# Softmax row sums of a hybrid attention block: the third pair of each batch is added to the sum tile by an accumulating transfer

## The chip, the cores and the metric

The kernel runs on one core of a Trainium2 chip. The core has a matrix engine (TensorE, "PE" in the profile; its weight loads are listed apart as "PEld"), a vector engine (VectorE, "DVE"), a scalar engine that evaluates activation functions (ScalarE, "ACT"), a general engine (GpSimd, "POOL") and an engine that feeds the DMA queue (SyncE, "SP"). Each engine works through its own instructions in order; between engines, semaphores say what may start. SBUF is the on-chip memory with 128 partitions, PSUM the memory that TensorE writes. The metric is the device time of one execution in microseconds.

## The reference

The reference is one layer of a diffusion backbone on 2048 latent tokens of width 1024 with 256 context tokens. Two head groups share one input projection: grouped-query softmax attention (8 query heads, 2 key heads, head dimension 64) and a bidirectional gated linear recurrence (4 heads of 128). Their outputs are concatenated and projected, and a SwiGLU feed-forward follows. The change is in the softmax attention:

```python
def block(q):
    s = jnp.einsum('bqkgd,bnkd->bkgqn', q, keys).astype(jnp.float32) * scale
    p = jax.nn.softmax(s, axis=-1)
    return jnp.einsum('bkgqn,bnkd->bqkgd', p.astype(vals.dtype), vals)

o = lax.map(block, qb)
```

Every query attends to 256 + 2048 = 2304 keys. The softmax needs, beside the weighted sum of the values, the sum of the exponentials over all 2304 keys, by which the result is divided.

## The kernel before

The kernel runs in stages: modulation vectors, the input projection (until about 730 us), the sweep of softmax attention with the recurrence woven into it (about 730 to 1738 us), the output projection, and the feed-forward in two halves.

The sweep goes through 32 items, one for each of the 16 blocks of 128 queries and each of the two key heads. An item has 4 query heads x 128 queries = 512 columns. For each of the 18 key tiles k of 128 keys, `scores` (lines 1000 and 1001) makes a tile `s` of 128 keys x 512 columns in PSUM with two matmuls, and ScalarE writes its exponentials to SBUF (line 1004, `p<-s`). Two neighbouring key tiles share one buffer `p` of 128 x 1024, a pair; there are six such buffers, and an item makes nine pairs.

Six key tiles, that is three pairs, form a batch (`BATCH = 6`): 32 items x 3 = 96 batches. When the fourth tile of a batch is done, GpSimd adds the first two pairs into the tile `ps` (`add`, line 1011; one buffer). The products of a batch are made at the end of the third step of the next batch (`LAGT = 3`), so two to three steps after the batch's last exponentials: first 12 matmuls with the values (line 1020, `av<-p,VS`), then the row sums (line 1028), in which a block of ones of 32 columns sums over the 128 keys. Line 1028 runs over two tiles: the sum `ps` of the first two pairs, and the third pair `p` as it is. Each is cut into 8 pieces of 128 columns, and four pieces go to four groups of 32 columns of TensorE side by side. All batches of an item add up in the columns 256 to 383 of the PSUM tile `av`, which `drain` empties once per item. In the profile a matmul on fp32 data stands as two records, so 8 products are 16 records.

Between the steps TensorE also makes the row minima for the next item (`mx`, line 969, read by DVE in line 971) and the matmuls of the recurrence (`pa`, line 684, and others). GpSimd works on the recurrence too: elementwise products `Q` (lines 715, 717), `M` (703), `C` (706) and others, on which TensorE and ScalarE wait.

In the sweep the order of TensorE and DVE, and of SyncE at its start, is that of the program text (`manual_schedule`). The order on ScalarE and GpSimd is set by a scheduler that lays the program out ahead of time by its own estimate of durations; waits are inserted where a tile is read or overwritten.

Of the kernel before, what the change touches and what calls it, by code (L numbers as in the profile page):

```python
# [13 lines left out]
ALU = mybir.AluOpType  # L14
AX = mybir.AxisListType

P = 128
# [51 lines left out]
def block_kernel(ctx: ExitStack, tc: tile.TileContext, a: dict, out: bass.AP, dbg=None):  # L69
    nc = tc.nc  # L70
# [78 lines left out]
    with ExitStack() as st:  # L149
# [11 lines left out]
        for j in range(8):  # L161
            wm = wmp.tile([P, KT, 256], F32, tag="wm", name=f"wm{j}")
            nc.sync.dma_start(wm, w_mod_r[:, :, j * 256:(j + 1) * 256])
            if j in DVE_MOD:
                for r in range(2):
# [5 lines left out]
                    for i in range(2):  # L171
                        nc.tensor.matmul(pcol[:, 2 * j + i, r:r + 1], acc[:, i * P:(i + 1) * P], ones,
                                         start=True, stop=True)
                continue
            pm = ps_m.tile([P, 512], F32, tag="mm", name=f"pm{j}", bufs=2)
            for k in range(KT):
                nc.tensor.matmul(pm[:2, :256], sc[:, k, :], wm[:, k, :],
                                 start=(k == 0), stop=(k == KT - 1))
# [33 lines left out]
    with ExitStack() as st:  # L212
# [40 lines left out]
        with ExitStack() as p1:  # L253
            ps_x = pool(p1, "ps_x", 4, PSUM)
            xh = pool(p1, "xh", 2)
            for gr in list(range(1, NTOK // 256)) + [0]:
# [6 lines left out]
                b = (gr + 1) // 2  # L263
                o = (gr - 1) % 2 * 256 if gr else 0
# [18 lines left out]
                for kk in range(KT // 2):  # L283
                    pt = ps_x.tile([P, 512], F32, tag="t", name=f"xT{gr}_{kk}")
                    for i in range(2):
                        for j, xt in enumerate(xs):
                            k = 2 * kk + i
# [3 lines left out]
                    for i in range(2):  # L291
                        k = 2 * kk + i
# [317 lines left out]
    with ExitStack() as st:  # L610
# [327 lines left out]
        NKT = NTOK // P  # L938
        BATCH = 6
        LAGT = 3  # L940

        class Item:
# [65 lines left out]
            def add(self, p):  # L1008

                t = self.sums[p // 3] = op.tile([P, 1024], F32, tag="ps", name=f"ps{self.nm}_{p}")  # L1010
                nc.gpsimd.tensor_tensor(t, self.pairs[p - 1], self.pairs[p], op=ALU.add)  # L1011

            def products(self, k0):

                if k0 == 0:
                    self.av = ps_av.tile([P, 512], F32, tag="av", name=f"av{self.nm}")
                for k in range(k0, k0 + BATCH):
                    for i in range(2):
                        o = k % 2 * 512 + i * 256
                        nc.tensor.matmul(self.av[i * 64:(i + 1) * 64, :256],  # L1020
                                         VS[:, k, self.g * 64:(self.g + 1) * 64],
                                         self.pairs[k // 2][:, o:o + 256],
                                         start=(k == 0), stop=(k == NKT - 1), skip_group_check=True)
                b = k0 // BATCH
                for n, t in enumerate((self.sums.pop(b), self.pairs[3 * b + 2])):
                    for o in range(0, 1024, 512):
                        for i in range(4):
                            nc.tensor.matmul(self.av[i * 32:(i + 1) * 32, 256:384], one32,
                                             t[:, o + i * P:o + (i + 1) * P], start=False,
                                             stop=(b == 2 and n == 1 and o > 0), skip_group_check=True)  # L1030

            def drain(self):
                self.ot = op.tile([P, 256], F32, tag="ot", name=f"ot{self.nm}")
# [18 lines left out]
        one32 = kvp.tile([P, 32], F32, name="one32")  # L1052
# [16 lines left out]
        items = [Item(g * NCH + qt, qt, g) for g in range(2) for qt in range(NCH)]  # L1069
# [28 lines left out]
        for x in range(NKT * NIT + 1):  # L1098
            n, k = divmod(x, NKT)
            item = items[n] if n < NIT else None  # L1100
            if item is None:
                rec.begin(2 * NIT)
                assert not chunks and not rec.lanes and not rec.plan and rec.late is None
                items[-1].products(NKT - BATCH)
                items[-1].drain()
                items[-1].finish(ps_st, "s")
# [59 lines left out]
                items[n - 1].drain()  # L1166
            for m, c in chunks.pop(x, ()):
                items[m].chunk(c)
            if rec.late is not None:
                wait -= 1  # L1170
                if wait <= 0:
                    rec.flush()
# [620 lines left out]
```

## Time and profile before

| what | value |
|---|---|
| median of 3 runs | 3235.79 us (3234.75 to 3237.18) |
| the profiled execution | 3230.49 us, its span 3228.7 us |
| mean granted TensorE clock | 0.993 of full speed |
| PE busy | 3145.3 us, 97% of the span |
| POOL busy | 1575.1 us, 49% |
| DVE busy | 1755.1 us, 54% |
| ACT busy | 1326.6 us, 41% |
| line 1011, POOL, the sums | 96 times, 2395 ns each |
| line 1028, PE, over the sums | 1536 records, 61.9 us |
| line 1028, PE, over the third pairs | 1536 records, 59.5 us |

How to read it: "x" behind an instruction is how often it is there. In the rows of groups, the busy time comes first, then the mean duration of one in ns, then the idle time of the engine just before and what ended it. In rows in order of time, the first number is the start and the second the duration in us; "x24" is a run of 24 merged into one row, and a bracket holds idle time before it and what ended it. Names like `ps<-p,p` give the tile that is written and those that are read, without buffer numbers. The busy time of a group counts overlapping instructions once, but two groups that overlap each other each count the shared time.

### The profile page before, as it was taken

What the parts mean: (1) busy time and instruction counts of PE and PEld (TensorE: products, weight loads), DVE (VectorE), ACT (ScalarE), POOL (GpSimd) and SP (SyncE); (2) the same over time, 40 slices, a digit from 0 to 9 for tenths busy, and PEclk for the clock granted to TensorE, in tenths of its full rate; (3) what the DMA queues carried; (4) which work ended last, traced back from release to release, by engine and by line L of the source; (5) the groups of instructions that cost most, each with busy time, mean ns of one, the idle gap of its engine ahead of it and who ended that gap; (6) DMA issues with size and microseconds to landing.
All of it is one profiled execution on the core that took longest, in us unless ns stands there. A gap on an engine that the chain in (4) does not pass through costs nothing. (4 is left out here: it accounts for less than half of the span.)

```text
span 3228.7 us, 55815 instructions
## 1 busy us (share of the span) xinstructions
PE 3145.3 (97%) x21212; PEld 2559.5 (79%) x21212; DVE 1755.1 (54%) x3070; ACT 1326.6 (41%) x2563; POOL 1575.1 (49%) x1403
## 2 busy tenths in 40 slices
PE   8999999999999999999999999999999999999998
PEld 5998987896777777777777887888877778888886
DVE  6344555416666665665653656445458753333566
ACT  4422222215554555554543225333335443333344
POOL 4322222206767767776634226777600168776222
PEclk9999999999999999999999999999999999999999
DMA  7243544324111211211006435555575533332665
GB/s 246 92 137 125 153 145 146 119 93 121 31 36 46 67 34 49 59 37 48 28 21 201 134 115 183 196 179 189 173 291 195 193 111 115 108 104 98 243 195 185
DMA packets 368999, 406.86 MB, mean 126 GB/s; under 512 B 31285, under 2 KB 260889, under 8 KB 368346
## 3 DMA queue, kind: packets, MB, share of 16 engines
q1 hardware_dynamic: 368730, 403.30, 38.9%
q8 instruction: 166, 2.72, 0.4%
q14 instruction: 103, 0.84, 0.1%
HBM read 273.34 MB, written 129.78 MB: 125 GB/s over the span
## 5 line engine op out<-in xcount | busy, mean ns | idle before, releaser
L971 DVE TENSOR_REDUCE mn<-mx 128x1 f32<-128x512 f32 x496 | 333.9, 685 | 209.7 <-PE mx L969 204.6
L1004 ACT ACTIVATE p<-s 128x512 f32<-128x512 f32 x576 | 338.5, 598 | 167.3 <-PE s L1001 147.5
L1011 POOL TENSOR_TENSOR ps<-p,p 128x1024 f32<-128x1024 f32 x96 | 229.9, 2395 | 162.3 <-ACT p L1004 162.3
L1020 PE MATMUL av<-p,VS 128*64 128x256 f32 x2304 | 268.7, 382 | 0.0
L1000 PE MATMUL s<-qa,K 128*128 128x512 f32 x576 | 253.4, 440 | 10.8 <-ACT p L1004 10.8
L1001 PE MATMUL s<-qb,KB 128*128 128x512 f32 x576 | 227.4, 395 | 0.0
L1020 PEld LDWEIGHTS av<-p,VS 128*64 128x64 f32 x2304 | 158.9, 138 | 82.5 <-issue 13.9
L969 PE MATMUL mx<-K,qa 128*128 128x512 f32 x496 | 200.9, 406 | 2.7 <-DVE mn L971 2.4
L1621 DVE TENSOR_TENSOR dl<-dl,x 128x512 fp32r<-128x512 f32 x154 | 113.7, 761 | 70.8 <-ACT x L1614 69.9
L1000 PEld LDWEIGHTS s<-qa,K 128*128 128x128 f32 x576 | 109.0, 189 | 47.9 <-issue 19.8
L1614 ACT ACTIVATE x<-dl 128x512 fp32r<-128x512 f32 x154 | 96.2, 631 | 106.1 <-DMA dl<-s_hid0A 41.1
L1614 ACT ACTIVATE dh<-dl 128x512 fp32r<-128x512 f32 x154 | 89.0, 623 | 93.7 <-PE pd1A L1682 48.3
L345 PE MATMUL f<-hTh,wh 128*128 128x512 f32 (+1 forms) x320 | 120.8, 377 | 6.9 <-ACT ft L374 6.9
L969 PEld LDWEIGHTS mx<-K,qa 128*128 128x128 f32 x496 | 93.4, 188 | 41.4 <-DVE mn L971 17.8
L1621 DVE TENSOR_TENSOR dl<-dl,dh 128x512 fp32r<-128x512 f32 x154 | 102.0, 688 | 43.1 <-ACT dh L1614 42.0
L122 POOL TENSOR_TENSOR rs_xf<-ms_xf,mhalf 128x1 f32<-128x1 f32 x16 | 12.7, 803 | 227.6 <-DVE ms_xf L120 227.6
L345 PE MATMUL f<-hTh,wl 128*128 128x512 f32 (+1 forms) x320 | 118.5, 370 | 0.0
L345 PE MATMUL f<-hTl,wh 128*128 128x512 f32 (+1 forms) x320 | 118.4, 370 | 0.0
L1001 PEld LDWEIGHTS s<-qb,KB 128*128 128x128 f32 x576 | 109.6, 190 | 10.9
L1445 PE MATMUL pA<-x,A22h 128*128 128x512 f32 x352 | 108.9, 391 | 4.5 <-DVE r L1518 4.5
L1445 PE MATMUL pA<-x,A11h 128*128 128x512 f32 x352 | 110.7, 395 | 2.4 <-ACT A11h L1414 2.4
L1445 PE MATMUL pC<-x,A12h 128*128 128x512 f32 x352 | 112.0, 391 | 0.0
(373 smaller groups left out, 9337.0 us busy)
## 6 DMA issues: line engine op xcount, KB each, us to landing
w<-in_w_gu_dram SPq DMA_DIRECT2D x88, 512.0 KB
wm<-in_w_mod_dram SPq DMA_DIRECT2D x24, 1024.0 KB
dl<-s_wT SPq DMA_DIRECT2D x88, 256.0 KB
dl<-s_wB SPq DMA_DIRECT2D x66, 256.0 KB
wq<-in_w_down_dram SPq DMA_DIRECT2D x44, 256.0 KB
s_wT<-wq SPq DMA_DIRECT2D x44, 256.0 KB
dl<-s_hid1S SPq DMA_DIRECT2D x44, 256.0 KB
dl<-s_hid0S SPq DMA_DIRECT2D x44, 256.0 KB
```

Source lines behind the costliest of these rows:

```text
L122: nc.gpsimd.tensor_tensor(rs, ms, mhalf[:, :width], op=ALU.pow)
L345: nc.tensor.matmul(pm[:, :n], w[wi][:, k, c0:c0 + P], hT[b][hi][:, k, :], start=(k == 0 and i == 0), stop=(k == KT - 1 and i == 2))
L969: nc.tensor.matmul(s, self.qa[:, h * P:(h + 1) * P], K[:, k * 512:(k + 1) * 512], start=True, stop=True)
L971: nc.vector.tensor_reduce(self.mn[:, h, k:k + 1], s, axis=AX.X, op=ALU.min)
L1000: nc.tensor.matmul(s, KS[self.g][:, ks], self.qa, start=True, stop=False)
L1001: nc.tensor.matmul(s, KB[k // BATCH][:, k % BATCH * P:(k % BATCH + 1) * P], self.qb, start=False, stop=True)
L1004: nc.scalar.activation(self.pairs[p][:, o:o + 512], s, AF.Exp, scale=-1.0)
L1011: nc.gpsimd.tensor_tensor(t, self.pairs[p - 1], self.pairs[p], op=ALU.add)
L1020: nc.tensor.matmul(self.av[i * 64:(i + 1) * 64, :256], VS[:, k, self.g * 64:(self.g + 1) * 64], self.pairs[k // 2][:, o:o + 256], start=(k ...
L1445: nc.tensor.matmul(acc, w[wi][:, k, :], x[xi][k], start=(start and k == 0 and i == 0), stop=(stop and k == KH - 1 and i == 2), skip_group_ ...
L1614: nc.scalar.activation(hi, f32v(lo), AF.Copy)
L1621: nc.vector.tensor_tensor(lo, f32v(lo), f32v(hi), op=ALU.subtract)
```

## The change

The third pair of each batch is no longer multiplied with ones by itself. Instead an accumulating transfer, issued from GpSimd's queue, adds it to the sum tile `ps` in SBUF: `ps += p`, 128 partitions x 1024 fp32 values, 512 KB. The products with ones then run over the one tile `ps`. The transfer is issued in the program text at the end of the first step of the next batch (`k % BATCH == 0`), and for the last batch of all just ahead of its products.

```diff
+            def add_last(self, p):
+
+                t = self.sums[p // 3]
+                nc.gpsimd.dma_start(t, self.pairs[p], accum_op=ALU.add)
+
             def products(self, k0):
...
                 b = k0 // BATCH
-                for n, t in enumerate((self.sums.pop(b), self.pairs[3 * b + 2])):
-                    for o in range(0, 1024, 512):
-                        for i in range(4):
-                            nc.tensor.matmul(self.av[i * 32:(i + 1) * 32, 256:384], one32,
-                                             t[:, o + i * P:o + (i + 1) * P], start=False,
-                                             stop=(b == 2 and n == 1 and o > 0), skip_group_check=True)
+                t = self.sums.pop(b)
+                for o in range(0, 1024, 512):
+                    for i in range(4):
+                        nc.tensor.matmul(self.av[i * 32:(i + 1) * 32, 256:384], one32,
+                                         t[:, o + i * P:o + (i + 1) * P], start=False,
+                                         stop=(b == 2 and o > 0), skip_group_check=True)
...
+                items[-1].add_last(NKT // 2 - 1)
                 items[-1].products(NKT - BATCH)
...
             for m, c in chunks.pop(x, ()):
                 items[m].chunk(c)
+            if k % BATCH == 0 and x:
+                items[(x - 1) // NKT].add_last((x - 1) % NKT // 2)
```

The places that count are the products with ones on TensorE and the sums on GpSimd. First TensorE, at the second batch of the 16th item (in the profile of before the one whose products with the values start at 1206.06 us). The rows give line, operation, tile written, tiles read and shape; the last number in a name is a running number, "x8" stands for eight instructions in a row. Before:

```order
L684 MATMUL pa_13692<-Q_12532,M_6_13577 64x64 x8
L1020 MATMUL av_0_13536<-p_0_3_13483,VS 64x256 x4
L1020 MATMUL av_0_13536<-p_0_4_13511,VS 64x256 x4
L1020 MATMUL av_0_13536<-p_0_5_13608,VS 64x256 x4
L1028 MATMUL av_0_13536<-ps_0_4_13591,one_7838 32x128 x8
L1028 MATMUL av_0_13536<-p_0_5_13608,one_7838 32x128 x8
L1000 MATMUL s_0_15_13759<-qa_0_12771,K_7830 128x512
```

And TensorE with the change at the same place (its lines are five further down in the file):

```order
L684 MATMUL pa_13371<-Q_12273,M_6_13255 64x64 x8
L1025 MATMUL av_0_13222<-p_0_3_13168,VS 64x256 x4
L1025 MATMUL av_0_13222<-p_0_4_13197,VS 64x256 x4
L1025 MATMUL av_0_13222<-p_0_5_13286,VS 64x256 x4
L1033 MATMUL av_0_13222<-ps_0_4_13269,one_7838 32x128 x8
L1000 MATMUL s_0_15_13430<-qa_0_12498,K_7830 128x512
```

Eight matmuls are gone; the others stand as before, and the products over `ps` directly behind those with the values, ahead of the next scores. Now GpSimd at the same batch, whose sum tile is `ps_0_4`, before:

```order
L665 TENSOR_TENSOR Q_13826<-q_13598,F_13596 128x512 x2
L1011 TENSOR_TENSOR ps_0_4_13591<-p_0_3_13483,p_0_4_13511 128x1024
L703 TENSOR_TENSOR M_3_13617<-M_2_13600,T_1_13606 128x16x2x4
L706 TENSOR_TENSOR C_3_13618<-M_2_13600,T_1_13606 128x16x8
L706 TENSOR_TENSOR C_4_13636<-M_3_13617,T_2_13623 128x8x16
L703 TENSOR_TENSOR M_4_13635<-M_3_13617,T_2_13623 128x8x2x8
```

And GpSimd with the change:

```order
L665 TENSOR_TENSOR Q_13498<-q_13276,F_13274 128x512 x2
L1011 TENSOR_TENSOR ps_0_4_13269<-p_0_3_13168,p_0_4_13197 128x1024
L703 TENSOR_TENSOR M_3_13295<-M_2_13278,T_1_13284 128x16x2x4
L706 TENSOR_TENSOR C_3_13296<-M_2_13278,T_1_13284 128x16x8
L1016 DMA ps_0_4_13269<-p_0_5_13286 128x1024
L706 TENSOR_TENSOR C_4_13314<-M_3_13295,T_2_13301 128x8x16
L703 TENSOR_TENSOR M_4_13313<-M_3_13295,T_2_13301 128x8x2x8
```

The transfer (line 1016) is a new row; here it stands two rows behind its sum, in 55 of the 96 batches directly behind it, and at most three rows of other work lie between. The recurrence's rows around it have moved by a few places at most.

## The prediction

> **What bounds the kernel now.** I read the page first (busy shares, slices, queues), then the stretch of the softmax sweep alone, then the groups of the two lines that the change touches, and last four neighbouring batches in order of time. The page:
>
> ```profile
> span 3228.7 us, 55815 instructions
> PE 3145.3 (97%) x21212; PEld 2559.5 (79%) x21212; DVE 1755.1 (54%) x3070; ACT 1326.6 (41%) x2563; POOL 1575.1 (49%) x1403
> PE   8999999999999999999999999999999999999998
> POOL 4322222206767767776634226777600168776222
> q1 hardware_dynamic: 368730, 403.30, 38.9%
> ```
>
> TensorE is busy in nine tenths of nearly every slice, GpSimd in six or seven tenths of the slices of the sweep (10th to 22nd). The only queue with data on it is the one that SyncE feeds: no transfer in this profile was issued by GpSimd, so the new instruction has no row of its own. The sweep, and in it the products with ones:
>
> ```profile
> 730.00:1738.00 1008.00, 981.89 (x10077) 732.57 (x10078) 600.90 (x1073) 519.81 (x1048) 683.62 (x718) 0.99 0.19 54
> 730.00:1738.00 1008.00, 103.77 (x3072) 77.99 (x3072) 0.99 0.19 54
> L1028 PE MATMUL av<-ps,one 128*32 128x128 f32 x1536 | 61.9, 279 | 0.0
> L1028 PE MATMUL av<-p,one 128*32 128x128 f32 x1536 | 59.5, 273 | 0.0
> L1011 POOL TENSOR_TENSOR ps<-p,p 128x1024 f32<-128x1024 f32 x96 | 229.9, 2395 | 162.3 <-ACT p L1004 162.3
>   POOL ps L1011: 0.4, 1
> ```
>
> The first row counts every engine (PE, PEld, DVE, ACT, POOL), the second only line 1028. The sweep has 96 batches in 1008 us, 10.5 us each, and TensorE works in 981.89 us of it: it sets the pace, and what is taken from it is gained. The last row is from the list of what line 1028 waited for: the products with ones waited for the sum in one batch of 96, for 0.4 us. The sum is on time, then, but a busy bar does not say by how much; that is the question here.
>
> **The change, part by part.**
>
> Removed: per batch one group of 16 recorded matmuls with ones, over the third pair. Its row says 59.5 us, but it overlaps the group over the sum: both together cover 103.77 us, the sum's group alone 61.9, so 103.77 - 61.9 = 41.9 us go. The time order gives the same from another side (rows below): in the batch at 1199 us the second group begins 0.46 us after the first (1199.25, 1199.71), as in the three others, and the next scores follow both at the same pitch; 96 x 0.46 = 44 us. I take 44, all of it on TensorE, which nothing hides. The dropped weight loads run beside the matmuls and count in it.
>
> Added: 96 transfers of 512 KB (128 partitions x 1024 fp32), which add the third pair onto the sum in SBUF. Each waits for two things, the end of the sum of the first two pairs (POOL, line 1011) and the exponentials of the batch's sixth tile (ACT, line 1004); and the products with ones, which now follow the transfer, stand on TensorE in the old place. So what counts is the room between the later of these two and the first product with ones. Four batches, with the rows that end each:
>
> ```profile
> 1191.00 2.40 POOL L1011 TENSOR_TENSOR ps<-p,p 128x1024 f32<-128x1024 f32 x1 [3.40 <-ACT p L1004]
> 1191.84 1.29 ACT L1004 ACTIVATE p<-s 128x512 f32<-128x512 f32 x2 [0.99 <-PE s L1001]
> ...
> 1199.25 0.64 PE L1028 MATMUL av<-ps,one 128*32 128x128 f32 x16
> 1199.71 0.62 PE L1028 MATMUL av<-p,one 128*32 128x128 f32 x16
> ...
> 1203.23 2.38 POOL L1011 TENSOR_TENSOR ps<-p,p 128x1024 f32<-128x1024 f32 x1
> ...
> 1206.06 2.76 PE L1020 MATMUL av<-p,VS 128*64 128x256 f32 x24
> ...
> 1208.75 0.65 PE L1028 MATMUL av<-ps,one 128*32 128x128 f32 x16
> ...
> 1214.19 2.42 POOL L1011 TENSOR_TENSOR ps<-p,p 128x1024 f32<-128x1024 f32 x1
> ...
> 1219.62 0.65 PE L1028 MATMUL av<-ps,one 128*32 128x128 f32 x16
> ...
> 1222.07 2.37 POOL L1011 TENSOR_TENSOR ps<-p,p 128x1024 f32<-128x1024 f32 x1 [1.32 <-ACT p L1004]
> ...
> 1224.59 0.59 ACT L1004 ACTIVATE p<-s 128x512 f32<-128x512 f32 x1
> ...
> 1231.54 0.65 PE L1028 MATMUL av<-ps,one 128*32 128x128 f32 x16
> ```
>
> First batch: sum done at 1191.00 + 2.40 = 1193.40, exponentials at 1193.13, products at 1199.25: room 5.85 us. Second: sum done 1205.61, products 1208.75: 3.14. Third: 1216.61 to 1219.62: 3.01. Fourth: here the exponentials are last, 1225.18, products 1231.54: 6.36. The mean is 4.6 us. The 24 matmuls of line 1020 (2.76 us) lie inside the room already. A transfer that takes L from the moment it may go to the moment the products may start costs, in each batch, L minus the room, if that is positive; TensorE's queue is in order, so all scores behind it slip by as much. I take the four for the 96 (times 24).
>
> What is L? The nearest rows are a load of the same 512 KB by SyncE into SBUF, at a quiet moment, its issue in order of time and then the windows (DMA share and GB/s are the last two columns):
>
> ```profile
> 768.01 0.33 SPq L643 DMA_DIRECT2D F<-s_f  x1
> 768.00:768.90 0.90, 0.52 (x6) 0.44 (x8) 1.00 0.00 0
> 768.90:770.50 1.60, 1.60 (x18) 1.06 (x16) 1.00 0.87 210
> 770.50:771.50 1.00, 0.64 (x6) 0.14 (x2) 1.00 0.49 197
> 771.50:772.00 0.50, 0.00 (x0) 0.00 (x0) 1.00 0.00 0
> ```
>
> The load is issued at 768.01 us; nothing moves until 768.90, and all has moved by 771.50: 0.9 us to the first byte and 2.6 us of movement, 3.5 in all. That is the lower end, a transfer that only copies. An accumulating one has two operands to fetch per element, its source and the sum; twice the movement is 5.2 us. The issue is bounded below by the same 0.9 us, above by the longest thing that GpSimd does with a tile of this size here, 2.4 us (line 1011). So L lies between 0.9 + 2.6 = 3.5 and 2.4 + 5.2 = 7.6, and more if the adding itself is slow. [...]
>
> [...]
>
> Lateness at L = 6.6: 0.75 + 3.46 + 3.59 + 0.24 = 8.04 us in four batches, 193 us in 96. At the ends: L = 3.5 gives 0.36 + 0.49 = 0.85, 20 us; L = 7.6 gives 12.04, 289 us.
>
> GpSimd's queue: 96 issues of 1.4 us are 134 us, 683.62 + 134 = 818 us of a sweep that gets 149 us longer (1157): 71%, still not the bound. In the order the transfer stands right behind its sum in 55 of the 96 batches, and the recurrence's work (Q, M, C) behind it, which waits through the issue and, as in the fourth batch, for 0.74 us of exponentials. TensorE's and ScalarE's recurrence steps wait for that work. The waiting of TensorE at the sums, some 2 us a batch, lets GpSimd catch up by about what the issues cost it, so I cost both at nothing together; if it caught up fully, the room would be that to the exponentials alone in the second and third batch too. The other way, an uncovered 1.4 us in every batch, is 134 us more at most.
>
> Single edits with one answer: the third pair's buffer is held until the transfer has read it, but TensorE read it last before, in the same place, and the products still follow; the sum's one buffer is free earlier or later only with the products; the stop flag moves to the last product and costs nothing. [...] SyncE's order is the same there but for a few rows at the sweep's end, and behind the sweep the order of work stays as it was.
>
> Sum: -44 + 193 = +149 us. The profiled execution took 3230.5 us, so 3379 for it; the median of the runs before is 5.3 us above it, 3235.8, and the forecast for the median is 3385.
>
> **The rivals.**
>
> *The transfer is hidden and the gain stays.* It needs L below 3.9 us: there the lateness, (3.9 - 3.14) + (3.9 - 3.01) = 1.65 times 24, is 40 us and nearly eats the 44. For it speaks the room of 5.85 and 6.36 in half the batches and the 3.5 us of the load; against it the second operand. At L = 3.5 the time is 3236 - 44 + 20 = 3212; where the second and third batch find a quicker GpSimd too, 3192.
>
> [...]
>
> *The adding is slow.* If the engines need longer than for two reads, say L = 9, the lateness is 3.15 + 5.86 + 5.99 + 2.64 = 17.6 a group of four, 423 us, and the time 3236 - 44 + 423 = 3615. No row speaks for or against it; only the other 512 KB transfers, all plain, lie at 2.6 us of movement.
>
> *GpSimd becomes the bound.* Per batch it works 683.62 / 96 = 7.1 us, and TensorE, relieved, (1008 - 44) / 96 = 10.0. An issue above 2.9 us on GpSimd would make its queue the pace. At 4 us, L is 9.2, the lateness 442 us and the time about 3634. The longest pass over such a tile (2.4 us) speaks against it.
>
> **How the numbers follow.** The forecast (L from 4.1 to 8): 0.61, own range 3242 to 3519. Hidden (faster): 0.13. Between them, L from 3.8 to 4.1, within 0.2%, which is about what a measurement of this kernel can tell from no change: 0.04. Slow adding: 0.18. GpSimd the bound: 0.04. Faster 0.13, same 0.04, slower 0.61 + 0.18 + 0.04 = 0.83. The range leaves out the hidden case and the far end of the slow ones: 3230 to 3630.
>
> **What would show it.** Right: the group av<-p,one is gone from TensorE, line 1028's cover falls by some 42 us, and the products with ones wait for a DMA into ps in most batches, some 2 us each, near 190 us together; scores and exponentials keep their durations; the sweep lasts some 1150 us and all other stages stay. Wrong: if these waits are a few us in total (hidden), if they average 4 us and more (slow adding), or if TensorE waits for Q or M of the recurrence instead and GpSimd's bar stands near ten tenths (its queue). What would make it wrong is above all the one number without a row, the time of an accumulating transfer.

## The result and the profile after

The changed kernel takes 3360.08 us (median of 4 runs, 3355.32 to 3366.92) against 3235.27 us before, measured beside it: a ratio of 1.0387, 95% interval 1.0372 to 1.0402, or 125 us more. The prediction was 3385 us. The profiled execution has a span of 3353.5 us at a granted clock of 0.980 (0.993 before). The page of the kernel after:

```profile
span 3353.5 us, 53042 instructions
PE 3144.7 (94%) x19676; PEld 2546.1 (76%) x19676; DVE 1761.7 (53%) x3070; ACT 1328.3 (40%) x2563; POOL 1655.0 (49%) x1499
PE   8999999988988889889888999999999999999998
q0 software_dynamic: 13824, 50.34, 8.0%
```

TensorE has 1536 records less and is yet busy as long as before (3144.7 us against 3145.3), so what is left became slower. The loss lies in the 9th to 22nd slices, the sweep, where eights stand among the nines. A new queue carries 50 MB, GpSimd's. The sweep alone, all engines and then line 1033 (the products with ones, line 1028 before):

```profile
730.00:1866.00 1136.00, 983.17 (x8563) 721.35 (x8563) 608.67 (x1074) 521.87 (x1049) 762.97 (x814) 0.96 0.41 93
730.00:1866.00 1136.00, 65.58 (x1536) 37.75 (x1536) 0.96 0.41 93
```

The sweep is 128 us longer (1136 against 1008), the whole of the loss. TensorE's idle time in it rose from 26.1 us (1008 - 981.89) to 152.8 (1136 - 983.17). What it waited for, from the list of waits of TensorE in the sweep (total us, times, longest), and the sources of those waits, from the groups by line and the transfers' own row:

```profile
PE av L1033 <- DMA ps<-p: 123.0, 63, 5.0
...
PE s L1000 <- ACT p L1004: 3.1, 3, 2.5
...
PE pk L732 <- POOL M L703: 2.0, 3, 1.0
```

```profile
L1016 POOL DMA_DIRECT2D ps<-p x96: 730/876/1065, 739.5 to 1851.6; - x96
DMA to landing us min/median/max: 4.4/4.8/8.6
```

The products with ones wait for the transfer in 63 of 96 batches, 2.0 us each; nothing else on TensorE's list is near. The issue holds GpSimd 0.88 us (the middle of the three durations, in ns), and the data has landed 4.8 us after it began. One batch in order of time, the same as the second of the prediction's four (there the sum began at 1203.23 and the products at 1208.75):

```profile
1272.88 2.37 POOL L1011 TENSOR_TENSOR ps<-p,p 128x1024 f32<-128x1024 f32 x1
1273.82 0.60 ACT L1004 ACTIVATE p<-s 128x512 f32<-128x512 f32 x1 [0.17 <-PE s L1001]
1275.04 2.76 PE L1025 MATMUL av<-p,VS 128*64 128x256 f32 x24
...
1275.62 0.46 POOL L706 TENSOR_TENSOR C<-M,T 128x128 f32<-128x128 f32 x1
1276.02 0.86 POOL L1016 DMA_DIRECT2D ps<-p  x1
1280.62 0.66 PE L1033 MATMUL av<-ps,one 128*32 128x128 f32 x16 [2.82 <-DMA ps<-p]
1281.21 0.80 PE L1000 MATMUL s<-qa,K 128*128 128x512 f32 x1
1281.80 0.63 PE L1001 MATMUL s<-qb,KB 128*128 128x512 f32 x1
```

The sum is done at 1275.25, the exponentials before that; the transfer is issued at 1276.02, behind work of the recurrence, and the products follow 4.60 us later, after 2.82 us in which TensorE had nothing to do. And the scores behind them, here 0.80 and 0.63 us, took about 0.4 us each at this place before. The windows around the batch, engine PE alone (busy, clock, DMA share, GB/s), tell why:

```profile
1277.60:1281.10 3.50, 0.68 (x18) 1.00 0.70 131
1281.10:1284.50 3.40, 3.40 (x16) 0.50 0.01 2
1284.50:1288.00 3.50, 2.53 (x14) 1.00 0.48 135
```

In the 3.4 us behind the wait TensorE is granted half its clock (the figure 0.50 in the second row). In the trace's clock record of the whole sweep there are 25 such stretches after, 99.0 us together, and 4 before (13.7 us). Each lasts 3.41 us or twice that. So the transfer costs twice: the wait, and then a stretch at half speed.

TensorE wasn't idle all through the time ahead of this stretch: in the first of these windows it worked for 0.68 of 3.50 us.

### The profile page after: what moved, and what is told of

Its sections match the earlier page's. It is cut to its first block, busy times and chain, and to the rows that moved or that the text cites. A ratio compares the mean times of both kernels' runs of the same rounds, so it can differ in the third digit from the quotient of the medians.

```text
span 3353.5 us, 53042 instructions
## 1 busy us (share of the span) xinstructions
PE 3144.7 (94%) x19676; PEld 2546.1 (76%) x19676; DVE 1761.7 (53%) x3070; ACT 1328.3 (40%) x2563; POOL 1655.0 (49%) x1499
## 5 line engine op out<-in xcount | busy, mean ns | idle before, releaser
L1000 PE MATMUL s<-qa,K 128*128 128x512 f32 x576 | 264.1, 459 | 3.1 <-ACT p L1004 3.1
L1001 PE MATMUL s<-qb,KB 128*128 128x512 f32 x576 | 236.5, 411 | 0.8 <-DMA qb<-mr 0.8
L969 PE MATMUL mx<-K,qa 128*128 128x512 f32 x496 | 207.9, 420 | 2.7 <-DVE mn L971 2.4
L1033 PE MATMUL av<-ps,one 128*32 128x128 f32 x1536 | 65.6, 291 | 123.1 <-DMA ps<-p 123.0
L1033 PEld LDWEIGHTS av<-ps,one 128*32 128x32 f32 x1536 | 37.7, 112 | 164.6 <-DMA ps<-p 157.3
L1453 PE MATMUL pB<-x,S1h 128*128 128x512 f32 x352 | 110.9, 396 | 2.3 <-ACT S1h L1422 2.3
```

The costliest lines, as they stand in the source:

```text
L969: nc.tensor.matmul(s, self.qa[:, h * P:(h + 1) * P], K[:, k * 512:(k + 1) * 512], start=True, stop=True)
L1000: nc.tensor.matmul(s, KS[self.g][:, ks], self.qa, start=True, stop=False)
L1001: nc.tensor.matmul(s, KB[k // BATCH][:, k % BATCH * P:(k % BATCH + 1) * P], self.qb, start=False, stop=True)
L1453: nc.tensor.matmul(acc, w[wi][:, k, :], x[xi][k], start=(start and k == 0 and i == 0), stop=(stop and k == KH - 1 and i == 2), skip_group_ ...
```

## Experiments

Four causes were open: the wait for the landing, the clock behind it, the work of GpSimd and its queue, and a gain smaller than the 44 us expected. In the tables below "half clock" is the sum of the half-clock stretches of the sweep in the profiled execution. Where a kernel leaves out or changes part of the sum, its exponentials have another scale (line 1004, `scale=-0.01` for `-1.0`), which changes no shape and no order. Differences in time are taken from the run of the kernel before that was measured beside each kernel (medians of 3232.67 to 3235.27 us). Where a kernel needs a tile more, the result `oo` is written over `ot` to make space; those lines aren't shown.

### The gain alone

```diff
-                items[-1].add_last(NKT // 2 - 1)
...
-            if k % BATCH == 0 and x:
-                items[(x - 1) // NKT].add_last((x - 1) % NKT // 2)
```

> The changed kernel without the transfer: the third pair of each batch is left out of the row sums, and the exponentials are taken with a hundredth of the scale (so that no sum is zero); all other work is as in the changed kernel. Theory A (the loss is the wait for the transfer's landing, and the slower clock behind long waits): the 42 us of the dropped products show in full, about 3193 us (3185 to 3202), no waits at the products with ones, and no more half-clock stretches in the sweep than the 4 of before. Rival B (the dropped products never were worth their time, because TensorE then waits for the recurrence on GpSimd): 3215 us or more, with waits for Q, M or C.

Measured: 3210.15 us, ratio 0.9928 (0.9913 to 0.9942), between the times of the two expectations. The dropped products are worth 24 us, not 44. The sweep, and new waits in it, of TensorE's weight loads and then of its matmuls:

```profile
730.00:1718.00 988.00, 951.56 (x8563) 696.65 (x8561) 605.21 (x1077) 517.54 (x1049) 681.79 (x718) 0.99 0.19 55
```

```profile
PEld pk L732 <- POOL M L703: 10.1, 3, 3.4
...
PE pk L732 <- POOL M L703: 8.8, 3, 2.9
```

The sweep is 20 us shorter. TensorE's busy time fell by 30.3 us (981.89 to 951.56), and its idle time rose by 10.3 (26.1 to 36.4), 8.8 of them in three waits for the tiles `M` of the recurrence: work that is off TensorE brings it sooner to these tiles, which GpSimd makes at its old pace (646 ns each on the mean, 649 before). Of the missing busy time (the group covered 41.9 us) some 5 us are the clock, an estimate: half of the 10.2 us by which the half-clock stretches rose (13.7 to 23.9). The rest isn't settled.

This run is also the base for the others: between it and the changed kernel, with the same 8563 records on TensorE, the sweep is 148 us longer, 116 us idle and 32 us of the same work done slower.

### The landing, by size

`half`, and `quarter` with 256 for 512:

```diff
-                nc.gpsimd.dma_start(t, self.pairs[p], accum_op=ALU.add)
+                nc.gpsimd.dma_start(t[:, :512], self.pairs[p][:, :512], accum_op=ALU.add)
```

> The accumulating transfer moves 256 KB instead of 512 KB: only the first half of the third pair is added, the second half is left out of the sums, and the exponentials are taken with a hundredth of the scale. Theory A1 (most of the 4.8 us to landing is movement of two operands): the landing falls to about 3.3 us, the waits at the products from 157 us to some 50, the time to about 3245 us (3220 to 3270). Theory A2 (most of it is a fixed cost of issue and completion): landing about 4.3 us, waits above 110 us, 3310 us or more. Rival B (GpSimd's queue, which the issue holds up): no change against the changed kernel if the issue stays at 0.88 us, 3350 to 3360.

> As the accumulating transfer of 256 KB, but 128 KB: a quarter of the third pair is added (the rest left out, a hundredth of the scale). 512 KB landed after 4.8 us, 256 KB after 3.4 us. If landing is a fixed part plus movement in proportion (2.0 + 1.4 per 256 KB): 2.7 us, and the time falls by half of the last step or a little less, to 3275 to 3295 us; what is then left above 3210 us is not movement but issue, completion and GpSimd's queue. If there is a floor under 256 KB: landing 3.2 us or more and 3295 to 3310 us.

| bytes | issue, us | landing (median), us | time, us | ratio (95%) | wait at the products, us | half clock, us |
|---|---|---|---|---|---|---|
| 512 KB (the changed kernel) | 0.88 | 4.8 | 3360.08 | 1.0387 (1.0372 to 1.0402) | 123.0 in 63 batches | 99.0 |
| 256 KB (`half`) | 0.88 | 3.4 | 3306.43 | 1.0222 (1.0207 to 1.0237) | 54.9 in 31 | 78.5 |
| 128 KB (`quarter`) | 0.88 | 2.7 | 3280.89 | 1.0141 (1.0121 to 1.0162) | 42.9 in 22 | 71.7 |

The issue costs GpSimd the same at every size; the landing is 2.0 us and 1.4 us more per 256 KB. The landing came out as the first theory of `half` had it, but the time lies outside its range, 3220 to 3270 us; `quarter` fell into its range. The time follows the landing: 124.8, 71.9 and 47.5 us above the kernel before. The first of these steps holds something else too: the smaller transfers read only the fifth tile of the batch, not the sixth, so they wait for less and are issued sooner (0.79 us behind the end of the sum on the mean, against 1.08). The second step has the size alone, and it is 35 us for each us of landing ((71.9 - 47.5) / 0.7). Carried on to 2.0 us, a transfer without data, that would be 23 us above the kernel before still, where the kernel without transfers lies 24 below: an estimate, but it says that some 45 us hang on something other than the size.

### A copy in place of the adding, from two queues

The sum goes to a tile of its own, and the transfer copies it to the tile that the products read: the same bytes and place in the program, but nothing is added. The copy waits for the sum only, not for the exponentials of the sixth tile. `plain_sp` issues it from SyncE (`nc.sync`).

```diff
-                t = self.sums[p // 3] = op.tile([P, 1024], F32, tag="ps", name=f"ps{self.nm}_{p}")
+                t = self.sums[p // 3] = op.tile([P, 1024], F32, tag="pu", name=f"pu{self.nm}_{p}")
...
-                t = self.sums[p // 3]
-                nc.gpsimd.dma_start(t, self.pairs[p], accum_op=ALU.add)
+                u = self.sums[p // 3]
+                t = self.sums[p // 3] = op.tile([P, 1024], F32, tag="ps", name=f"ps{self.nm}_{p}")
+                nc.gpsimd.dma_start(t, u)
```

> The transfer copies instead of adding: from GpSimd's queue, 512 KB from the sum of the first two pairs into a second tile, over which the products with ones run; the third pair is left out of the sums, and the exponentials are taken with a hundredth of the scale. The product of item output is written over its own input tile to make room for the second tile. It waits for the sum only, not for the sixth exponentials. Theory A1 (reading a second operand and adding costs most): landing near the 3.5 us of the SyncE load, waits some 50 us, time about 3240 us (3215 to 3265). Theory A2 (issue and completion from this queue cost most): landing 4.3 us or more, time above 3310 us.

> As the copying transfer of 512 KB from GpSimd's queue (third pair left out of the sums, a hundredth of the scale), but issued by SyncE. Theory A (landing against room): SyncE's transfer lands in about 3.0 us too, so the waits stay near those of the copy from GpSimd, 3265 to 3295 us. Rival B (the instruction on GpSimd's queue, 0.6 us, and what it holds up): without it the time falls below 3250 us.

Measured: 3285.36 us from GpSimd's queue, ratio 1.0154 (1.0137 to 1.0171), and 3239.50 us from SyncE's, 1.0020 (1.0009 to 1.0030). The transfer's row and the products' wait, from GpSimd:

```profile
L1017 POOL DMA_DIRECT2D ps<-pu x96: 567/593/767, 739.9 to 1784.8; - x96
...
DMA to landing us min/median/max: 2.9/3.0/8.6
```

```profile
PE av L1034 <- DMA ps<-pu: 57.1, 35, 3.9
```

And from SyncE:

```profile
PE av L1034 <- DMA ps<-pu: 27.7, 26, 2.4
```

Both times lie outside what the first theory of each gave; the second of `plain_sp` held. Without the adding the same 512 KB land in 3.0 us, not 4.8, and 74 of the 125 us are gone. Not all 74 are the landing's: the copy is also issued sooner, 0.68 us behind the end of the sum on the mean where the adding transfer takes 1.08, which at 35 us for each us is an estimate of 14 us, and its issue is shorter (0.59 us for 0.88). The packets show the difference in landing: in the trace's records one of 4 KB takes 0.340 us when it is added and 0.162 us when it is copied (medians).

Issued by SyncE the copy costs 44 us less (50.8 - 6.8). Some 29 of them are shorter waits at the products (57.1 to 27.7). Where the products waited, they came 3.0 us behind the issue in both runs (medians 3.03 and 3.05), so the landing is no quicker; but from GpSimd the issue came 0.68 us behind the end of the sum on the mean, from SyncE 0.09. On GpSimd it stands in one order with the sums and the recurrence's work. The other 15 can't be put to one wait. No accumulating transfer was issued from SyncE, so whether the change itself could go that way wasn't tried.

### The transfers without the wait

The kernel of the first experiment, and 96 accumulating transfers of the same size and place into a tile of zeros that nobody reads:

```diff
-                t = self.sums[p // 3]
-                nc.gpsimd.dma_start(t, self.pairs[p], accum_op=ALU.add)
+                nc.gpsimd.dma_start(spare_sum, self.pairs[p], accum_op=ALU.add)
```

> The kernel without the transfer (third pair left out of the sums, a hundredth of the scale), and beside it the 96 accumulating transfers of 512 KB from GpSimd's queue, now into a tile that nobody reads, so that no engine but GpSimd's own next transfer waits for a landing (an item's output is written over its input tile to make room). The run without the transfer took 3210 us. Theory A (the loss is the wait for the landing and the clock that it slows): 3210 to 3222 us. Rival B (the issue on GpSimd's queue and the recurrence's work held up behind it are a good part of the loss): 3235 us or more, with waits of TensorE for Q, M or C. The copy of 512 KB took 46 us more from GpSimd's queue than from SyncE's, which speaks for a part of B.

Measured: 3250.11 us, ratio 1.0046 (1.0034 to 1.0058), so 41 us more than without the transfers (16.7 above the kernel before, not 24.4 below), though no product waits for a landing. The sweep, two of TensorE's waits in it, and a group of GpSimd, in that order:

```profile
730.00:1749.00 1019.00, 959.65 (x8549) 701.43 (x8548) 605.57 (x1073) 516.04 (x1047) 757.75 (x814) 0.97 0.45 102
```

```profile
PEld s L1000 <- ACT p L1004: 27.5, 25, 4.3
...
PE s L1000 <- ACT p L1004: 19.2, 12, 3.9
```

```profile
L703 POOL TENSOR_TENSOR M<-M,T 128x256 f32<-128x256 f32 (+1 forms) x120 | 84.0, 700 | 0.8 <-DVE T L721 0.7
```

The same group without transfers (`no_transfer`):

```profile
L703 POOL TENSOR_TENSOR M<-M,T 128x256 f32<-128x256 f32 (+1 forms) x120 | 77.5, 646 | 1.5 <-DVE T L721 1.4
```

GpSimd is busy 76 us longer than without the transfers (757.75 to 681.79). That is the issues, 0.87 us each at the middle, and slower rows, such as the products `M`, which take 700 ns instead of 646; the two overlap in part. TensorE meets it later and at other places, above all as scores that wait for ScalarE (19.2 us where the run without transfers has 11.5). Of the 41 us, 31 lie in the sweep: 23 idle and 8 of slower work (59.4 - 36.4, 959.65 - 951.56). Which of the two, the issues or the slower rows, weighs more stays open. A third is in this run too, the traffic: the DMA engines are busy for 0.45 of the sweep instead of 0.19, and ScalarE and GpSimd wait 12 us more for the loads of `F` (17.4 and 7.7 us, 10.6 and 2.1 without transfers). No run parts it from the others, so the 41 us are those of the transfers apart from the wait, not shown to be GpSimd's alone. They are close to the 45 us that the sizes left over.

### More room for the transfer

The products with ones are made three steps later, with two sum tiles; `drain` and `finish` move by as much. `before_room3` is the same move in the kernel before, without the transfer.

```diff
-                t = self.sums[p // 3] = op.tile([P, 1024], F32, tag="ps", name=f"ps{self.nm}_{p}")
+                t = self.sums[p // 3] = op.tile([P, 1024], F32, tag="ps", name=f"ps{self.nm}_{p}", bufs=2)
...
+            def row_sums(self, k0):
...
-            if k == 3 and n:
+            if k == 6 and n:
                 items[n - 1].drain()
...
-            if k == 5 and n:
+            if k == 8 and n:
                 items[n - 1].finish(ps_h, "h")
...
+            y = x - 5 - BATCH
+            if k % BATCH == 5 and y >= 0:
+                items[y // NKT].row_sums(y % NKT)
```

> The changed kernel's whole computation, with its products with ones three steps later (at the end of the sixth step of the next batch instead of the third, two sum tiles instead of one, the emptying of the item three steps later as well; the item's output is written over its input tile to make room). Theory A (landing against room): three steps are some 3 us more room, so nearly all waits at the products go, with them the long gaps and the half-clock stretches; time 3190 to 3215 us, below the kernel before. Rival B (the issue on GpSimd's queue and what it holds up behind it): the queue is as it was, so the loss stays, above 3300 us.

> The kernel before, whole, with its products with ones three steps later, as in the run that moves them in the changed kernel (two sum tiles, the emptying of an item three steps later, the output written over its input tile). If moving the products is itself free: 3230 to 3240 us, and the 3255 us of the moved changed kernel are the transfer's own cost. If the later products or the later emptying cost by themselves: 3250 us or more, and the remaining loss there is not the transfer's.

Measured: 3255.55 us with the transfer, ratio 1.0072 (1.0054 to 1.0091); 3241.38 us for the kernel before with the same move, 1.0026 (1.0015 to 1.0037). Waits of TensorE with the transfer:

```profile
PE av L1035 <- DMA ps<-p: 18.2, 20, 2.5
...
PE pk L732 <- POOL M L703: 15.9, 3, 5.3
```

None of the expected times was met. The same transfer, landing as late (4.7 us), loses 104 of its 125 us when the products come three steps later. So the wait, with the half clock behind it (41.0 us of it left for 99.0), was the cause of most of it. But the kernel doesn't become faster than before: of the 21 us left the move itself costs 9 (by the second run), and the transfer 12 beyond that, though the dropped products bring 24. If these parts simply add, that is a cost of some 36 us with most of the waits gone, the third figure beside the 45 and the 41; 18.2 us of waits are still in it.

### The clock

If the half clock comes from TensorE's idle time, work that nobody needs, put into that time, should bring the clock back. `filler` puts 32 unread matmuls (some 1.8 us) ahead of the products with ones in the 19 batches with the longest gaps, `filler2` 56 of them (`range(14)`) in 42 batches.

```diff
+                if 3 * self.n + b in FILL:
+                    for j in range(8):
+                        for i in range(4):
+                            nc.tensor.matmul(self.av[i * 32:(i + 1) * 32, 384:512], one32, VS[:, 0, :],
+                                             start=False, stop=False, skip_group_check=True)
```

> The changed kernel, whole, with 32 further matmuls of 128 columns (some 1.8 us), whose results nobody reads, ahead of the products with ones in the 19 batches whose gap on TensorE was 2.4 us or more. If the half-clock stretches come from the length of those gaps: the gaps fall below 2.8 us, the half-clock stretches of the sweep from 25 to 8 or fewer, and the time falls by 20 to 40 us although work was added, 3320 to 3340 us. If the clock has nothing to do with the gaps: as many stretches as before and 3360 us or more.

> The changed kernel, whole, with 56 further matmuls of 128 columns (some 3.2 us), whose results nobody reads, ahead of the products with ones in the 42 batches whose gap on TensorE was 1.2 us or more. The first such run cut the gaps by 1.8 us and left the half-clock stretches; in the traces each stretch follows a fixed window of 3.41 us in which TensorE was busy for less than about half. If the clock goes by that busy share: nearly no window falls below it, and the half-clock stretches of the sweep go from 25 to 6 or fewer; the added work costs about 40 us where the gap was shorter than it, the clock gives back about 30: 3350 to 3380 us. If the stretches stay at 20 or more, the share is not what sets them.

Measured: 3371.33 us, ratio 1.0420 (1.0399 to 1.0442), and 3397.04 us, 1.0501 (1.0469 to 1.0532). With the first, 24 stretches were left of 25: the length of the gap, on which it was built, was a poor reading. In the traces of before and after, the clock record changes only on a fixed grid of 3.41 us. Laid against it, the stretches of the kernel before followed windows in which TensorE was busy for 0.32 to 0.34 of the time, and the lowest window that led to none had 0.57. In the changed kernel the two overlap: of the windows at full clock, those that led to one had up to 0.52, and the lowest that led to none had 0.41. In the sweeps of all runs every window at full clock below 0.40 led to a stretch and none above 0.55 did; between them it went either way. A window that itself ran at half clock could lead to another at more, up to 0.84 (in `half`). So the busy share of the window is what the stretches go by as far as the traces show, but it alone doesn't fix a boundary. By that reading a gap of 2.8 us that is split evenly between two windows may do nothing (it leaves 0.59 of each, an estimate from 1.4 of 3.41 us), and a filling of 1.8 us, 0.53 of a window, may not lift one that holds little else far enough. The second run, with more, left 13 stretches (47.8 us for 99.0), more than expected, in a time above the expected range; but for one that went on from a half-clock window, they followed windows of 0.53 and less. That agrees with the reading but doesn't prove it. Neither kernel gained: in the second TensorE is busy 117.5 us longer in the sweep and idle only 78.5 us less, so the unread work is longer than the idle time that it fills and the clock that it gives back.

### The adding on another engine

```diff
-                nc.gpsimd.dma_start(t, self.pairs[p], accum_op=ALU.add)
+                nc.vector.tensor_tensor(t, t, self.pairs[p], op=ALU.add)
```

The call stands just ahead of the products. `dve_late` does this in the last 5 of the 32 items only (15 batches, with 32 of the recurrence's `Q`, `M` and `C` products left on GpSimd) and leaves the others as in the kernel before.

> The third pair is added onto the sum tile by VectorE (one elementwise addition of 128x1024 per batch, standing just ahead of the batch's products) instead of by the transfer; the products are those of the changed kernel and the whole result is computed. Theory A (what lost the time is the landing, not the dependence on a second addition): an addition on VectorE takes some 1.2 us by the two of that shape in the next stage (1.23 us), less than the 2.8 us of products that cover it, so the time comes near that of the kernel without the transfer, 3205 to 3230 us, below the kernel before. Rival (a later sum is bad in itself, because VectorE waits for GpSimd's sum and the minima behind it are held up): 3240 us or more.

> The kernel before, whole, but in the last 5 of the 32 items (15 batches), where little of the recurrence is left on GpSimd, the third pair is added to the sum tile by VectorE ahead of the products, and those run over one tile; the other 27 items are as before. If the dropped products pay wherever the addition is off the engines that are needed: 15 x (24 / 96 to 42 / 96 us) = 4 to 7 us less, 3226 to 3230 us against 3233. If the addition on VectorE costs there too: 3233 us or more.

Measured: 3249.25 us, ratio 1.0048 (1.0030 to 1.0067), which is the time that the rival gave, and 3231.92 us, 0.9998 (0.9986 to 1.0009), no difference that shows (the interval leaves room for a gain of 4 us, not of 7). In the first:

```profile
730.00:1752.00 1022.00, 961.72 (x8557) 701.27 (x8557) 728.69 (x1171) 512.03 (x1048) 749.45 (x718) 0.98 0.19 53
```

```profile
L715 POOL TENSOR_TENSOR Q<-Q,T 128x256 f32<-128x256 f32 x96 | 101.0, 1052 | 75.9 <-PE pa L684 75.8
```

And the same group without the adding (`no_transfer`):

```profile
L715 POOL TENSOR_TENSOR Q<-Q,T 128x256 f32<-128x256 f32 x96 | 66.7, 694 | 80.9 <-PE pa L684 80.9
```

VectorE has the time for it (busy 728.69 of 1022 us). But GpSimd, with the same 718 instructions as without the adding, is busy 749.45 us instead of 681.79; its products `Q` take 1052 ns instead of 694. The trace tells where: the 43 of them that overlap an addition on VectorE in time took 1481 ns, the other 53 705. Why they took longer, the trace doesn't show. TensorE is idle 24 us longer than in `no_transfer`; 15.5 of them are scores that wait for ScalarE (27.0 us, 11.5 there), and 7.3 are products that wait for the addition itself, in 9 batches. So this way too is paid for, for the most part away from the products; that it goes through the recurrence's path is argued from GpSimd's longer rows. No version tried that makes the whole sum beats the kernel before by more than the noise.

## Why the prediction was right, and where not

The sign, the mechanism (products that wait for a DMA into `ps`) and the time within 25 us held. The terms did so less well, and the nearness is in part luck: the waits were taken 70 us too long, and a gain taken 20 us too large and two terms that were missing made up for most of it.

| term | predicted, us | shown, us | by |
|---|---|---|---|
| products gone | -44 | -24 | `no_transfer` |
| waits for the landing | +193 | 123 | the list of waits after |
| GpSimd's issues and its queue | 0 | about +40, traffic included | `side_transfer`, also `room3`, the sizes |
| clock behind the waits | not in the sum | at most 32 of slower work, some 8 of it in the line above | windows of the sweep |
| sum | +149 | +125 | the runs |

The terms shown are measured in different runs and overlap, so they don't add up to the last line. From `no_transfer` on, the loss is 124.8 + 24.4 = 149 us, of which 41 come with transfers that nobody waits for; if the rest is the wait, 108 belong to the waiting and the clock behind it.

**The room.** The step that took four batches for 96, with the room between the later of sum and exponentials and the first product, was sound. With the L that the trace shows, about 0.5 us from ready to issue (the median) and 4.8 to the landing, 5.3 us together, the prediction's own formula gives (5.3 - 3.14 + 5.3 - 3.01) x 24 = 107 us; the rooms of all batches in the trace of before give 111 us, in 57 batches, so the four were a fair sample. 123 were measured, in 63 batches rather than 48.

**L.** The term that was mis-sized is L, 6.6 us taken: 1.4 us until the first byte and 5.2 of movement, twice the load's 2.6. These were estimates; no run of before shows a transfer from GpSimd's queue or one that adds. The first part measured 1.45 us from the issue; but the issue came 0.5 us behind the moment at which it could go, and the landing is told 0.34 us behind the end of the last packet, two parts that the estimate had no term for. The second had about the right factor (0.340 us for a packet that is added against 0.162 for one that is copied; what in the adding takes the time, no run shows) but the wrong base: the 2.6 us were those of a load from HBM, and the copy inside SBUF from this queue moved in 1.5 us (from its first byte, 1.17 us after the issue, to the end of its last packet). The movement took 3.0 us where 5.2 were taken:

```profile
1276.00:1276.90 0.90, 0.90 (x3) 1.00 0.02 1
1276.90:1277.60 0.70, 0.70 (x3) 1.00 0.50 94
1277.60:1280.40 2.80, 2.80 (x7) 1.00 0.88 164
1280.40:1281.00 0.60, 0.60 (x3) 1.00 0.00 0
```

These are windows of the kernel after, engine POOL, with DMA share and GB/s last, for the transfer issued at 1276.02.

**The gain.** "All of it on TensorE, which nothing hides" failed: 24 us came of 44. Of the 20 that are missing, the trace of `no_transfer` gives 8.8 to TensorE's waits for GpSimd's `M` and some 5 to the half clock; the rest stays open. That a pace-setter's time is gained in full holds only as long as no other engine's result is waited for instead.

**GpSimd.** "I cost both at nothing together" failed by some 40 us, the transfers' traffic included; the bound named beside it, 134 us, held. Its cover was to be TensorE's waiting at the sums, but `side_transfer`, where no product waits, and `room3`, where few do, can't lean on it, and the copy on SyncE's queue, where they still wait 27.7 us, was 44 us better.

**What was to be seen.** The group over the third pair is gone, and line 1033's cover is 65.58 us for 103.77, 38 us less (42 forecast); most batches wait, 2.0 us each, but 123 us together and not near 190; the sweep lasts 1136 us (1150 forecast), and the other stages stay. "Scores and exponentials keep their durations" didn't hold for the scores. The groups of their two lines on TensorE, of the kernel after:

```profile
L1000 PE MATMUL s<-qa,K 128*128 128x512 f32 x576 | 264.1, 459 | 3.1 <-ACT p L1004 3.1
L1001 PE MATMUL s<-qb,KB 128*128 128x512 f32 x576 | 236.5, 411 | 0.8 <-DMA qb<-mr 0.8
```

They took 253.4 and 227.4 us before. That is the half clock, which the prediction had no term for: at full clock the two take 438 and 394 ns on the mean, as before (440 and 395), at half clock 683 and 618.

**The rivals.** Hidden: refuted in this place, L is 5.3 us, above the 3.9 that it needed. Slow adding: refuted as priced, a packet took 0.340 us when it was added and 0.162 us when it was copied, some twice the time and not more. GpSimd the bound: refuted as a pace (763 of 1136 us busy), but on a small scale it has a part in the 41 us. Two readings in the prediction are off, and nothing rests on them: GpSimd's bar has three and four tenths in the last two slices of the sweep, and with L = 3.8 its sum gives 9 us less, 0.3%, and not within 0.2%.

## What to carry to other kernels

A transfer on the path is costed from its issue to its landing, with the operation it does (here 4.8 us for 512 KB added, 3.0 for the same copied) and the memories it goes between (2.6 us of movement for the load, 1.5 for the copy inside SBUF), and against the room in each batch: here every us of landing was worth some 35 us, an estimate from `half` and `quarter`. To take work off the engine that sets the pace pays only until it waits for another engine instead (here 24 us came of 44), so ask who is second, and be slow to give that engine the new work; here even the issuing of a copy was 44 us cheaper from SyncE than from GpSimd. And the gaps on TensorE counted twice here, where enough of them fell into one window of 3.41 us: beside 123 us of waits stood at most 32 us of slower work, so a wait should be priced with the slower work behind it.

## What the runs showed of the hardware

- An accumulating transfer of fp32 inside SBUF landed 2.7, 3.4 and 4.8 us after its issue began, for 128, 256 and 512 KB (in these three, 2.0 us plus 1.4 us per 256 KB); the same 512 KB as a copy from the same queue took 3.0 us. A packet of 4 KB took 0.340 us when it was added and 0.162 us when it was copied.
- Issuing held GpSimd 0.88 us for an accumulating transfer at each of these sizes, and 0.59 us for a copy of 512 KB; SyncE needed 0.50 us (its row's median) for that copy.
- With the accumulating transfers about, GpSimd's `M` rows took 700 ns instead of 646 on the mean in `side_transfer`, and 712 in the changed kernel. By the median they took 669, 670 and 666 ns for 512, 256 and 128 KB with the products waiting, 652 without transfers, so the amount moved made no difference that shows; with the copies from the same queue the mean was 638. Why isn't known.
- A `Q` row of GpSimd that overlapped an addition of two SBUF tiles on VectorE took 1481 ns (43 rows of `dve`) instead of 705 (the other 53).
- TensorE's half clock came in steps of 3.41 us, behind fixed windows of that length. In the sweeps of these runs it came behind every window at full clock in which TensorE was busy for less than 0.40, behind none above 0.55, and either way between; one of them had 0.52 in the changed kernel, so a window needn't be idle. The 25 stretches in the sweep, against 7 without the transfers, came with 32 us of slower work in a sweep of the same 8563 records on TensorE.
